# The mixer of a two-layer hybrid decoder: TensorE's order written out while tracing, 64-row scores in pairs

## The chip, the cores and the metric

The kernel runs on one NeuronCore of one Trainium2 chip. The metric is device time in microseconds (us) of one execution. PE is TensorE, PEld its weight loads, DVE VectorE, ACT ScalarE, POOL GpSimd and SP SyncE, whose queue issues most of the transfers.

## What is computed

Two layers on a residual stream of 512 positions by 1024 features in float32; each has a SwiGLU feed-forward stage (FFN), a token mixer and a second FFN, all with RMSNorm and a shift, scale and gate from a conditioning vector. The reference, cut:

```python
for l in range(DEPTH):                              # DEPTH = 2
    h = modulate(rms_norm(x, norm_g[l, 0]), sh1, sc1)
    x = x + 0.5 * g1 * swiglu(h, w_ffn_gu[l, 0], w_ffn_down[l, 0])      # 1024 -> 2 x 2816 -> 1024
    h = modulate(rms_norm(x, norm_g[l, 1]), sh2, sc2)
    x = x + g2 * token_mixing(h, w_in[l], w_out[l], ...)
    h = modulate(rms_norm(x, norm_g[l, 2]), sh3, sc3)
    x = x + 0.5 * g3 * swiglu(h, w_ffn_gu[l, 1], w_ffn_down[l, 1])
return rms_norm(x, final_norm_g)

def token_mixing(h, ...):
    (hq, hf, hi, hg, aq, ak, av, iq, ik, iw, sz, sxbc, sdt) = split(h @ w_in)
    o_a = hgrn2_mixer(hq, hf, hi, hg, ...)          # 4 heads of 64, gated linear recurrence
    o_b = dsa_mixer(aq, ak, av, iq, ik, iw, ...)    # 8 index heads pick the 128 best keys of each query, 4 heads attend
    o_c = mamba2_mixer(sz, sxbc, sdt, ...)          # conv of 4 taps, 8 heads of 64, state 128
    return concatenate([o_a, o_b, o_c]) @ w_out     # 256 + 256 + 512 features
```

## The kernel before

The stream lives in SBUF as eight tiles `X[f]` of 128 features by 512 positions. A dense product is split for accuracy (`mm3`, L304): operands are cut into a high part (`hi`, the rounded type fp32r) and the rest (`lo`), and PE sums hi·hi, lo·hi and hi·lo, three matmuls of 512 columns per 128 by 128 weights. `weights` (L294) loads a chunk of 1024 columns on SP's queue (`wraw`), ACT copies `whi`, DVE subtracts `wlo` (L301); three buffers of each.

Each stage begins with `lead` (L254): two chunks are multiplied by the not yet normalised stream (`xhi`, `xlo`), while the sum of squares is formed; behind product k = `KR[0]` PE sums it over partitions (`msps`), behind `KR[1]` it spreads the result (`rsb`, copied to `rb`). DVE then makes, tile by tile, `ht` = X·gain·rb (L283) and the low part `hlo` (L289), ACT the high part `hhi` (L284). The shift of the two chunks comes as a separate vector: DVE sums eight weight blocks, each by its shift column, into `shw` (L261), and PE reduces it (`pb`, L274).

`mixer` (L444) multiplies by 18 feature-major chunks of `winF` (`fm`, tile `pf`: query 0–1, index query 2–5, forget 6–7, hgrn query 8–9, conv input 10–17) and by position-major groups `winB`, `winV`, `winG`, `winC` (`tm_group`, tile `pt`). Around these:

- *topk* (L536): index scores `ipl`, 24 matmuls with 64 rows each, ACT's Relu, DVE's weighted sum into `iacc` (L550); then 3 x 16 rounds of MAX8 and MATCH_REPLACE8 on DVE.
- *hgrn* (L606): diagonal scores `ldg`, then seven levels of block size 64 to 1. A level makes two tiles `lev` (one for each 128 features; DVE, exponential on ACT, products on POOL) and 16 matmuls `lsc` of 64 rows and 128 columns (L667): four blocks of positions for each head half `par` and tile `f`, in four PSUM tiles; DVE copies them under a mask into `asc` (L669). The two heads of a tile lie in its rows 0–63 and 64–127; `par` is the outer loop, so four matmuls on the same half follow each other.
- *attend* (L743): for each block j of 128 queries and each head a 64-row score `apl`, maximum on DVE, exponential on ACT, transposes `apt`, product `apo`.
- *ssd* (L781): decays (`prow`, `mt`: eight Relu pieces, L839), outputs (`pyd`, `pyo`, `pst`); then `ysplit` (transposes `pyt`) and `project` (`po`).

`zipped` (L729) merges the generators by fixed fractions; that sets priorities, and a list scheduler with a cost model then decides the order on each engine, on PE too, apart from the lead. PSUM has eight banks: three for `mm`, three for `sm`, two for `hm`. `SLOTS` counts the SBUF buffers of each kind.

## Time and profile before

| | us |
|---|---|
| median of 3 runs | 2138.05 |
| lowest and highest run | 2138.03, 2138.57 |
| span of the profiled execution | 2136.6 |

| stretch of layer 0 (us of the span) | what runs |
|---|---|
| 48–404 | first FFN, end of the start-up |
| 399–412 | lead of the mixer, under the last products of the FFN and its own |
| 412–487 | winB, rotations, first chunks of winF |
| 487–610 | levels, index scores, top-k, conv input |
| 610–678 | gates, attention, state space part |
| 678–715 | end of attention and of the state space part, last projection |
| from 715 | second FFN |

Layer 1 has its mixer from 1442.5 to 1758.5. The profiled execution's own time is its span and what lies around it; the table of the runs gives the whole. Of the page, read the busy shares and the chain first, then the timeline of a stretch; busy time of PE is modelled from the starts of its matmuls, so that starts are the safer number. In the rows a matmul of float32 operands stands as two passes, so that a block of eight is x16.

### The profile page before, as it was taken

To read this page: it belongs to the slowest core of one execution; us is meant where nothing else is said; L and a number is where in the kernel's file an instruction comes from. 1 tells how busy PE (TensorE), PEld (TensorE's weight loads), DVE (VectorE), ACT (ScalarE), POOL (GpSimd) and SP (SyncE) were. 2 spreads that over 40 slices of the span, in tenths; PEclk is the share of its full clock that TensorE was granted. 3 is DMA by queue.
4 is the path that set the end of the run, shared out by engine and by line. 5 is a ranking of instruction groups with operands and counts; after the bars stand their busy time and mean duration, and the time that the engine had idled before them with its cause. 6 is when DMAs were issued, how large, how long until landed. Compare 5 with 4: busy or idle time off the path is not lost.

```text
span 2136.6 us, 26813 instructions
## 1 busy us (share of the span) xinstructions
PE 2084.7 (98%) x10201; PEld 1724.8 (81%) x10201; DVE 1304.8 (61%) x2540; ACT 817.7 (38%) x1245; POOL 201.1 (9%) x178
## 2 busy tenths in 40 slices
PE   4999999999999999999999999999999999999998
PEld 3888888887888788888888888888779877888886
DVE  8766564769986877433476743357699775333333
ACT  4422223455564532222342222234655644222233
POOL 4000000112221200000100000011123120000001
PEclk9999999999999999999999999999999999999999
DMA  8556563432110367432346743233311023233322
GB/s 307 204 194 234 179 209 89 128 104 65 58 31 15 121 204 263 129 99 84 94 139 222 273 155 99 78 106 110 94 55 43 16 72 99 90 88 114 94 84 73
DMA packets 103537, 262.51 MB, mean 123 GB/s; under 512 B 12272, under 2 KB 14960, under 8 KB 103408
## 3 DMA queue, kind: packets, MB, share of 16 engines
q1 hardware_dynamic: 100016, 256.60, 37.6%
q10 hardware_dynamic: 3392, 4.20, 0.7%
q8 instruction: 80, 1.31, 0.3%
q14 instruction: 49, 0.40, 0.1%
HBM read 255.50 MB, written 2.10 MB: 121 GB/s over the span
## 4 chain that ended last, share of the span: by engine, by line
PE 94%; DVE 4%; DMA 1%; issue 1%; ACT 1%; SPq 0%; DVEq 0%; ACTq 0%
PE pd L305 7%; PE pd L307 7%; PE pd L306 7%; PE pg L305 7%; PE pu L307 7%; PE pg L306 7%; PE pu L305 7%; PE pu L306 7%; PE pg L307 7%; PE pf L305 3%; PE pf L307 3%; PE pf L306 3%; PE lsc L667 3%; PE pt L469 2%; PE pt L471 2%; PE pt L470 2%
## 5 line engine op out<-in xcount | busy, mean ns | idle before, releaser
L300 ACT ACTIVATE whi<-wraw 128x1024 fp32r<-128x1024 f32 (+2 forms) x374 | 356.7, 957 | 978.3 <-issue 335.2
L301 DVE TENSOR_TENSOR wlo<-wraw,whi 128x1024 fp32r<-128x1024 f32 (+2 forms) x374 | 412.3, 1103 | 389.1 <-ACT whi L300 387.7
L306 PE MATMUL pd<-alo,whi 128*128 128x512 f32 (+1 forms) x715 | 275.8, 386 | 0.0
L307 PE MATMUL pd<-ahi,wlo 128*128 128x512 f32 (+1 forms) x715 | 275.8, 386 | 0.0
L305 PE MATMUL pd<-ahi,whi 128*128 128x512 f32 (+1 forms) x715 | 275.5, 386 | 0.0
L307 PE MATMUL pu<-hhi,wlo 128*128 128x512 f32 x664 | 258.6, 390 | 1.6 <-DVE wlo L301 1.6
L305 PE MATMUL pu<-hhi,whi 128*128 128x512 f32 x664 | 258.7, 390 | 0.2
L305 PE MATMUL pg<-hhi,whi 128*128 128x512 f32 x664 | 258.6, 390 | 0.0
L306 PE MATMUL pu<-hlo,whi 128*128 128x512 f32 x664 | 258.4, 389 | 0.0
L307 PE MATMUL pg<-hhi,wlo 128*128 128x512 f32 x664 | 258.3, 389 | 0.0
L306 PE MATMUL pg<-hlo,whi 128*128 128x512 f32 x664 | 258.3, 389 | 0.0
L160 DVE SCALAR_TENSOR_TENSOR adaw<-adaw,crow 128x512 f32<-128x512 f32 x288 | 193.2, 710 | 5.2 <-DMA adaw<-wada 5.0
L199 POOL TENSOR_TENSOR sq<-sq 128x512 f32<-128x512 f32 x36 | 53.9, 1496 | 1421.4 <-ACT sq L195 1421.2
L396 DVE TENSOR_TENSOR a<-a,pu 128x512 f32<-128x512 f32 x85 | 58.4, 687 | 201.6 <-PE pu L307 201.6
L307 PEld LDWEIGHTS pd<-ahi,wlo 128*128 128x128 f32 x715 | 134.3, 188 | 27.1
L306 PEld LDWEIGHTS pd<-alo,whi 128*128 128x128 f32 x715 | 134.3, 188 | 27.0
L305 PEld LDWEIGHTS pd<-ahi,whi 128*128 128x128 f32 x715 | 134.3, 188 | 27.0
L307 PEld LDWEIGHTS pu<-hhi,wlo 128*128 128x128 f32 x664 | 124.7, 188 | 28.7 <-DVE wlo L301 2.9
L305 PEld LDWEIGHTS pu<-hhi,whi 128*128 128x128 f32 x664 | 124.6, 188 | 27.1 <-ACT whi L300 1.5
L307 PEld LDWEIGHTS pg<-hhi,wlo 128*128 128x128 f32 x664 | 124.6, 188 | 26.0
L305 PEld LDWEIGHTS pg<-hhi,whi 128*128 128x128 f32 x664 | 124.7, 188 | 25.8
L306 PEld LDWEIGHTS pu<-hlo,whi 128*128 128x128 f32 x664 | 124.6, 188 | 25.8
(305 smaller groups left out, 3361.1 us busy)
## 6 DMA issues: line engine op xcount, KB each, us to landing
wraw<-wgu SPq DMA_DIRECT2D x176, 512.0 KB, 3.6
adaw<-wada SPq DMA_DIRECT2D x288, 256.0 KB, 5.0
wraw<-wdn SPq DMA_DIRECT2D x64, 384.0 KB, 3.1
wraw<-wdn SPq DMA_DIRECT2D x64, 320.0 KB, 2.9
wraw<-winF SPq DMA_DIRECT2D x36, 512.0 KB, 3.6
wraw<-woutB SPq DMA_DIRECT2D x16, 384.0 KB, 3.1
wraw<-winC SPq DMA_DIRECT2D x8, 512.0 KB, 3.6
rope<-rraw ACTq DMA_DIRECT2D x48, 64.0 KB, 3.8
```

The source lines that it names most:

```text
L160: V.scalar_tensor_tensor(raw, raw, 1.0, crow[:, h], op0=OP.mult, op1=OP.mult, accum_out=part[:, c, h:h + 1])
L199: (eng if f < NF - 1 else V).tensor_add(ssq_t["t"][:, h], ssq_t["t"][:, h], sq[:, h])
L300: ACT.activation(hi, raw, AF.Copy)
L301: V.tensor_sub(lo, raw, hi.bitcast(F32))
L305: PE.matmul(ps, wh, xh, start=first, stop=False)
L306: PE.matmul(ps, wh, xl, start=False, stop=False)
L307: PE.matmul(ps, wl, xh, start=False, stop=last)
L396: V.tensor_mul(a, a, pu)
L469: PE.matmul(o, hh[kk][:, blk(b)], wh[:, wk], start=first, stop=False, **g)
L470: PE.matmul(o, hl[kk][:, blk(b)], wh[:, wk], start=False, stop=False, **g)
L471: PE.matmul(o, hh[kk][:, blk(b)], wl[:, wk], start=False, stop=last, **g)
L667: PE.matmul(ps[:, blk(b)], xl[f][ph, blk(b)], xl[f][ph, blk(b)], start=True, stop=True)
```

## The change

It touches the mixer, its lead and the pools; the products and their number stay as they are.

- **PE's order.** The whole mixer is under a manual schedule of PE (`mixer_woven`). `weave` runs one generator `dense()` and five chains (`topk`, `hgrn`, `attends`, `ssd`, `select`). A chain yields the time at which it may go on; `clk` advances by the issued PE time (`tick`, 0.681 per `mm3`). `need` waits for marks with latencies, `need_pair` for a PSUM pair; a chain that is due goes ahead of the dense products. The clock is used while tracing only; on the chip PE runs the list in its order.
- **Dense order.** Forget and hgrn query ('h'), winB and index queries ('i'), queries ('q'), winV ('v'), conv ('c'), then winC0, winC1, winG and woutA.
- **Pairs.** `pair` is a tile of two PSUM banks, two buffers; `mm` and `sm` go to two banks each, `hm` goes. `head_pair` sends the matmuls of rows 0–63 and 64–127 alternately into the two banks; `ipl` and `apl` do the same with two or four heads.
- **Merged tiles.** `lev`, `lf`, `kf`, `hq`, `bf`, `kd`, `asc` hold both feature tiles, [128, 2, 512]; a level takes one set of vector instructions.
- **Engines.** `wlo` of 12 winF chunks (`GF`) moves to POOL. The weighted sum of the index scores is ACT scaling plus POOL addition. The lead's `shw` is a POOL product of the whole chunk and one DVE reduction. `KR` goes to (4, 5), in all stages.
- Smaller: state tiles cleared once, norms per block, first level copied by ACT, the start's tiles, a smaller DMA scratch ring.

```diff
-KR = (3, 4)
+KR = (4, 5)
...
-ZD, ZH, ZQ, ZC, ZG = (0.18, 0.59), (0.04, 0.86), (0.04, 0.63), (0.06, 0.79), (0.89, 0.94)
+SPACE = 1.6
+LEVLAT = 9.0
+ATTLAT = 10.0
...
+DORD = 'hiqvc'
...
+SLOTS = {"H": 16, "A": 14, "B": 9, "C": 18}
 WBUF = 3
+GF = (6, 7, 8, 9, 10, 11, 12, 13, 14, 15, 16, 17)
...
         def sm(name, shape=(P, S)):
-            return pq.tile(list(shape), F32, name=name, tag="sm", bufs=3)
-
-        def hm(name, shape=(P, S)):
-            return pq.tile(list(shape), F32, name=name, tag="hm", bufs=2)
+            return pq.tile(list(shape), F32, name=name, tag="sm", bufs=2)
+
+        def pair(name):
+            return pq.tile([P, 2, S], F32, name=name, tag="pair", bufs=2)
...
             with tc.high_priority(WAHEAD):
                 for wh, wl, raw in ws:
-                    t = act("A", "shw", shape=(P, P))
-                    V.tensor_scalar(t, raw[:, blk(0)], shift_of(l, i, 0), None, op0=OP.mult)
-                    for q in range(1, NF):
-                        V.scalar_tensor_tensor(t, raw[:, blk(q)], shift_of(l, i, q), t, op0=OP.mult, op1=OP.add)
-                    ts.append(t)
+                    r4 = raw.rearrange("p (a b m) -> p a b m", a=4, b=2)
+                    GP.tensor_tensor(r4, r4,
+                                     mod[l][:, i * 6:i * 6 + 4, 1::2][:, :, :, None].to_broadcast([P, 4, 2, P]),
+                                     op=OP.mult)
+                    r = act("A", "shw", shape=(P, P))
+                    V.tensor_reduce(r, raw.rearrange("p (q m) -> p m q", q=NF), axis=AX.X, op=OP.add)
+                    ts.append(r)
...
-        def weights(src, n, keep=False):
+        def weights(src, n, keep=False, eng=None):
...
                 ACT.activation(hi, raw, AF.Copy)
-                V.tensor_sub(lo, raw, hi.bitcast(F32))
+                (eng or V).tensor_sub(lo, raw, hi.bitcast(F32))
...
+        def weave(dense, chains):
+            when = lambda e: e[0]() if callable(e[0]) else e[0]
+            src, todo = [0.0, dense], [[0.0, g] for g in chains]
+            while src or todo:
+                live = todo + ([src] if src else [])
+                e = next((e for e in live if when(e) <= clk[0]), None)
+                if e is None:
+                    e = min(live, key=when)
+                    assert when(e) < math.inf
+                    clk[0] = when(e)
+                r = next(e[1], e)
+                if r is not e:
+                    e[0] = r if callable(r) else clk[0] + (r or 0.0)
+                elif e is src:
+                    src = None
+                else:
+                    todo.remove(e)
+
         def mm3(ps, wh, wl, xh, xl, first, last):
+            tick(0.681)
             PE.matmul(ps, wh, xh, start=first, stop=False)
             PE.matmul(ps, wh, xl, start=False, stop=False)
             PE.matmul(ps, wl, xh, start=False, stop=last)
...
+            iqp = pair("pq")
+            iqp = [iqp[:, c] for c in range(2)]
             hh, hl, sb, rb = lead(l, 1, [weights(A["winF"][l, 2 + c], 1024, True) for c in range(2)], iqp)
+            with tc.manual_schedule(engines={mybir.EngineType.PE}):
+                mixer_woven(l, nxt, iqp, hh, hl, sb, rb)
+
+        def mixer_woven(l, nxt, iqp, hh, hl, sb, rb):
...
+            b3 = lambda t: t.rearrange("p (b t) -> p b t", b=NB)
+
+            def mark(k, lat):
+                at[k] = clk[0] + lat
+
+            def need(*ks):
+                return lambda: max(at.get(k, math.inf) for k in ks)
+
+            def need_pair(t=0.0):
+                return lambda: max(t, min(pfree))
+
+            def hold_pair(lat):
+                pfree[pfree.index(min(pfree))] = clk[0] + lat
 
...
                 ps = mm("pf")
                 for k in range(NF):
                     mm3(ps, wh[:, blk(k)], wl[:, blk(k)], hh[k], hl[k], k == 0, k == NF - 1)
+                    yield
                 return ps
...
+            def dense():
+                hold_pair(16.0)
+                for c in DORD:
+                    yield from dict(h=d_forget, i=d_index, q=d_query, v=d_value, c=d_conv)[c]()
                 sz[:] = [act("C", "sz") for _ in range(NB)]
                 for half in range(2):
-                    pC = tm_group(f"winC{half}", 256, 4)
...
+                sg[:] = [act("C", "sg", shape=(P, 2, 256)) for _ in range(2)]
+                yield from tm_group("winG", 256, 4, lambda bp, pp: ACT.activation(sg[bp], pp, AF.Silu))
+                mark("sg", 2.0)
+                yield from first_out()
...
+                        for i in range(hs):
+                            ph = slice(i % 2 * 64, i % 2 * 64 + 64)
+                            PE.matmul(pl[:, i % 2, i // 2 * n:i // 2 * n + n], iqr[(h + i) // 2][ph, blk(j)],
+                                      ikT[ph, :n], start=True, stop=True)
+                        tick(0.2 + n * hs / 1200)
+                        hold_pair(2.5)
...
+                            rl = act("A", "irl")
+                            ACT.activation(rl[:, :hs // 2 * n], pl[:, u, :hs // 2 * n], AF.Relu)
+                            for i in range(hs // 2):
...
+                                r = rl[:, i * n:i * n + n]
+                                if h + i + u == 0:
+                                    ACT.activation(acc[:, :n], r, AF.Copy, scale=w)
+                                else:
+                                    ACT.activation(r, r, AF.Copy, scale=w)
+                                    GP.tensor_tensor(acc[:, :n], acc[:, :n], r, op=OP.add)
...
+            def head_pair(name, kx, qx):
+                ps = pair(name)
+                for b in range(NB):
+                    for u in range(2):
+                        ph = slice(u * 64, u * 64 + 64)
+                        PE.matmul(ps[:, u, blk(b)], kx[ph, blk(b)], qx[ph, blk(b)], start=True, stop=True)
+                tick(1.15)
+                hold_pair(HOLD)
+                return ps
...
+                    for f in range(2):
+                        yield need_pair(ready + 2.0 * f)
+                        ps = head_pair("lsc", xl[:, f], xl[:, f])
+                        if m == 64:
+                            ACT.activation(b8(Asc[f])[:m, :, m:], b8(ps)[:m, :, m:], AF.Copy)
+                        else:
+                            w = lambda t: t.rearrange("p f (g u m) -> p f g u m", u=2, m=m)[:, :, :, 1]
+                            mk = masks[:, li].rearrange("p (g m) -> p g m", m=m)
+                            V.copy_predicated(w(Asc[f]), mk[:, None].to_broadcast([P, 2, S // (2 * m), m]), w(ps))
+                        if f == 0 and li + 1 < len(LEVELS):
...
+                        pl = pair("apl")
+                        for i in range(hs):
+                            ph = slice(i % 2 * 64, i % 2 * 64 + 64)
+                            PE.matmul(pl[:, i % 2, i // 2 * n:i // 2 * n + n], aqr[(h0 + i) // 2][ph, blk(j)],
+                                      akT[ph, :n], start=True, stop=True)
...
-                    px = mm("pxs")
+                    yield need_pair(clk[0] + 2.0)
+                    pr = pair("prow")
+                    for g in range(2):
+                        for r in range(4):
+                            h = g * 4 + r
+                            PE.transpose(pr[:, g, blk(r)], acs[:, b, h:h + 1].to_broadcast([P, P]), ident)
+                    tick(0.9)
+                    hold_pair(4.0)
+                    yield need_pair()
...
+            chains = dict(t=topk, h=hgrn, a=attends, s=ssd)
+            weave(dense(), [chains[c]() for c in ORD] + [select()])
```

Where instructions stand now. PE behind the lead of the first mixer, before and then after (`pb` is the shift sum, `pt` here winB, `pf` a winF chunk):

```order
L307 MATMUL pf<-xhi,wlo 128x512
L274 MATMUL pb<-ones,shw 128x1 x2
L469 MATMUL pt<-whi,hhi 128x208
L470 MATMUL pt<-whi,hlo 128x208
L471 MATMUL pt<-wlo,hhi 128x208
```

```order
L346 MATMUL pq<-xhi,wlo 128x512
L289 MATMUL pb<-ones,shw 128x1 x2
L344 MATMUL pf<-hhi,whi 128x512
L345 MATMUL pf<-hlo,whi 128x512
L346 MATMUL pf<-hhi,wlo 128x512
...
L542 MATMUL pt<-whi,hhi 128x208
```

Ninety-six winF products (four chunks of 24) now stand where winB's began; winB comes behind them.

PE at the level of block size 64, before and then after (`lsc` level scores, `ipl` index scores, `pf` and `pt` dense products):

```order
L305 MATMUL pf<-hhi,whi 128x512
L667 MATMUL lsc<-lev 128x128 x4
L543 MATMUL ipl<-kT,rope 128x384 x2
L667 MATMUL lsc<-lev 128x128 x4
L306 MATMUL pf<-hlo,whi 128x512
L307 MATMUL pf<-hhi,wlo 128x512
```

```order
L544 MATMUL pt<-wlo,hhi 128x208
L749 MATMUL lsc<-lev 128x128 x8
L344 MATMUL pf<-hhi,whi 128x512
L345 MATMUL pf<-hlo,whi 128x512
L346 MATMUL pf<-hhi,wlo 128x512
L749 MATMUL lsc<-lev 128x128 x8
```

Eight level scores on alternate halves stand together, three dense products lie between the two blocks of a level, and index scores stand elsewhere.

POOL from the last level on, before and then after (`kf`, `hq` hgrn key and query, `iacc` index sums, `wlo` low part of winF chunks, `dsd` a diagonal of the state space part):

```order
L660 TENSOR_TENSOR lev<-lev,hq 128x256
L678 TENSOR_TENSOR kf<-kf,lev 128x512
L684 TENSOR_TENSOR hq<-hq,bf 128x512
L816 TENSOR_SCALAR dsd<-ident,vec_77 128x128 x4
...
L706 MEMSET hst 128x128 x5
```

```order
L316 TENSOR_TENSOR wlo<-wraw,whi 128x1024
L720 TENSOR_TENSOR iacc<-iacc,irl 128x384
L804 TENSOR_TENSOR kf<-kf,lev 128x1024
L806 TENSOR_TENSOR hq<-hq,bf 128x1024
L720 TENSOR_TENSOR iacc<-iacc,irl 128x384
L316 TENSOR_TENSOR wlo<-wraw,whi 128x1024
L720 TENSOR_TENSOR iacc<-iacc,irl 128x384 x3
L721 TENSOR_TENSOR iacc<-iacc,cst 128x128
```

Additions of the index scores and subtractions of weights alternate on POOL, and the products for `kf` and `hq` stand between them.

PE near the end of attention (j = 3), before and then after (`apo` attention output, `apl` scores, `prow` and `pxc` decays, `py` and `pyd` state space output, `po` the projection):

```order
L765 MATMUL apo<-kv,pT 128x64 x4
L750 MATMUL apl<-kT,rope 128x512
L836 MATMUL prow<-ident,acs 128x128 x8
L306 MATMUL po<-ylo,whi 128x512
L307 MATMUL po<-yhi,wlo 128x512
...
L307 MATMUL po<-yhi,wlo 128x512
L848 MATMUL pyd<-dsd,xbc 128x128
L851 MATMUL pyd<-xdt,mt 128x64 x2
```

```order
L916 MATMUL apo<-kv,pT 128x64 x8
L885 MATMUL apl<-kT,rope 128x512 x2
L977 MATMUL prow<-ident,acs 128x128 x8
L984 MATMUL pxc<-ident,xbc 128x128 x4
L988 MATMUL pxc<-xbc 128x128 x2
L993 MATMUL pxc<-ident,xbc 128x128 x2
L1017 MATMUL py<-dsd,xbc 128x128
L1020 MATMUL py<-xdt,mt 128x64 x2
```

The decays of a block and its output now follow each other with no dense product between them; `prow`, `pxc` and `py` are three users of the two pairs.

## Rows read from the trace of the kernel before

**Rows 1.** The page: busy time and share of the span, granted clock, chain by engine.

```profile
PE 2084.7 (98%) x10201; PEld 1724.8 (81%) x10201; DVE 1304.8 (61%) x2540; ACT 817.7 (38%) x1245; POOL 201.1 (9%) x178
...
PEclk9999999999999999999999999999999999999999
...
PE 94%; DVE 4%; DMA 1%; issue 1%; ACT 1%; SPq 0%; DVEq 0%; ACTq 0%
```

**Rows 2.** PE's timeline (start, us, line, operation): mixer 0's ends, its sums of squares.

```profile
399.25 0.39 PE L305 MATMUL pf<-xhi,whi 128*128 128x512 f32 x1
...
403.33 0.95 PE L227 MATMUL msps<-ones,sq 128*128 128x1 f32 x8
...
715.34 0.39 PE L305 MATMUL pg<-xhi,whi 128*128 128x512 f32 x1
```

**Rows 3.** Stretches: us, busy PE, PEld, DVE, ACT, POOL, clock, DMA share, GB/s.

```profile
404.00:487.00 83.00, 81.82 (x464) 70.75 (x464) 53.89 (x105) 45.88 (x63) 11.01 (x7) 1.00 0.35 104
487.00:610.00 123.00, 122.97 (x759) 99.54 (x756) 120.80 (x293) 68.93 (x114) 34.02 (x36) 1.00 0.19 55
...
678.00:723.00 45.00, 42.20 (x195) 33.10 (x194) 36.97 (x57) 20.82 (x31) 11.53 (x7) 1.00 0.29 89
```

**Rows 4.** The chain of waits (start us, us, what), score blocks on PE.

```profile
487.38 0.88 PE ldg L645 x8
...
532.85 1.98 PE lsc L667 x16
...
614.52 0.84 PE apl L750 x2
...
639.81 1.05 PE apl L750 x2
```

**Rows 5.** Timeline of PE, and of weight loads (PEld): passes on both and one half.

```profile
486.68 0.70 PE L543 MATMUL ipl<-kT,rope 64*128 64x256 f32 x4
...
525.40 0.19 PEld L667 LDWEIGHTS lsc<-lev 64*128 64x128 f32 x1
525.40 0.19 PEld L543 LDWEIGHTS ipl<-kT,rope 64*128 64x128 f32 x1
...
608.44 0.70 PE L750 MATMUL apl<-kT,rope 64*128 64x256 f32 x2
```

**Rows 6.** PE's timeline at one level block.

```profile
532.46 0.40 PE L306 MATMUL pf<-hlo,whi 128*128 128x512 f32 x1
532.78 2.05 PE L667 MATMUL lsc<-lev 64*128 64x128 f32 x16
```

**Rows 7.** Timeline behind the lead of mixer 0: DVE, PE and POOL.

```profile
408.49 0.75 DVE L289 SCALAR_TENSOR_TENSOR hlo<-ht,mod,hhi 128x512 fp32r<-128x512 f32 x1
...
409.83 0.75 DVE L289 SCALAR_TENSOR_TENSOR hlo<-ht,mod,hhi 128x512 fp32r<-128x512 f32 x1
...
411.94 0.35 PE L469 MATMUL pt<-whi,hhi 128*128 128x208 f32 x1
...
413.35 0.28 PE L469 MATMUL pt<-whi,hhi 128*128 128x208 f32 x1
...
421.67 1.78 POOL L486 TENSOR_TENSOR rraw<-rraw,cst 128x512 f32<-128x512 f32 x1 [16.09 <-DMA rope<-rraw]
...
422.22 1.78 DVE L289 SCALAR_TENSOR_TENSOR hlo<-ht,mod,hhi 128x512 fp32r<-128x512 f32 x1
```

**Rows 8.** Groups by line and form (busy us, mean ns): DVE from 404 to 746, POOL overall.

```profile
L301 DVE TENSOR_TENSOR wlo<-wraw,whi 128x1024 fp32r<-128x1024 f32 x31 | 38.4, 1238 | 15.1 <-ACT whi L300 15.1
L669 DVE COPY_PREDICATED asc<-masks,lsc 128x256 f32<-128x256 uint8 x28 | 14.3, 510 | 0.9 <-PE lsc L667 0.9
...
L550 DVE SCALAR_TENSOR_TENSOR iacc<-irl,kv,iacc 128x512 f32<-128x512 f32 x7 | 5.5, 780 | 0.0
...
L362 POOL TENSOR_TENSOR wlo<-wraw,whi 128x512 fp32r<-128x512 f32 x4 | 6.0, 1531 | 11.8 <-ACT whi L361 11.8
```

**Rows 9.** The same view of ScalarE, from 404 to 746.

```profile
L839 ACT ACTIVATE mt<-prow,acs 128x128 f32<-128x128 f32 x32 | 9.1, 379 | 3.0 <-PE prow L836 3.0
```

715 lines of the change are left out of this document (391 added, 324 removed).

## The prediction

> **What bounds the kernel now.** I read the page first. TensorE (PE) is busy 98% of the span at the upper of its two clocks (2.4 GHz: 9 tenths or more granted in every slice, 1.00 in the stretches of [rows 3]), and the chain that ended last is 94% PE [rows 1]. So the time is a queue of matmuls, and only a change in PE's time or in PE's waits can show. Next the timeline of PE, to cut out one mixer: from its first product to the first product of the FFN behind it 715.34 - 399.25 = 316.1 us [rows 2]; the second mixer is the same code on other weights, so every term below counts twice. The 18 products from 399.25 to the sum of squares at 403.33 give the price of a dense product of 512 columns, 0.227 us. Then the table by stretch: from 404 to 610 PE idles 1.2 us of 206, and VectorE (DVE) is busy 120.80 of the 123 us in which the levels and the top-k run, while GpSimd (POOL) has 34 of them [rows 3]. Thus PE has almost no waits to remove. DVE only just keeps up there.
>
> **What is removed from PE.** A score matmul works on 64 of the 128 rows. The chain shows what one block of eight costs when it stands alone: 1.98 us for 16 passes (each such matmul is two), and the attention scores 0.84 us for 384 columns and 1.05 us for 512 [rows 4]. Do two on opposite halves run side by side? The timeline shows it by chance: four 256-column index passes, of two heads that use the two halves, take 0.70 us, and two passes of one half take 0.70 us too; and at 525.40 two weight loads of the two halves start together [rows 5]. After the change every head pair alternates halves. Per mixer:
> - level scores: 7 levels x 16 matmuls = 14 blocks of eight, 14 x 1.98 = 27.7 us, halved: -13.9;
> - diagonal scores: 16 matmuls, four runs of 0.88, 3.5 us, halved: -1.8;
> - attention scores: 16 matmuls, four heads each of 1.05 and 0.84 us, and of 0.6 and 0.4 for 256 and 128 columns (an estimate: in proportion 0.55 and 0.27, and something for the ends), 11.6, halved -5.8, less 0.3 for ends that stay: -5.5;
> - index scores: 24 matmuls, 20 us if each stood alone, but most already stand beside another (first row of [rows 5]); half of what is left, an estimate: -3.5 (2 to 10 by how many do);
> - a block between dense products costs more than its passes: the block follows the product before it after 0.32 instead of 0.227 us [rows 6], and as much again is lost behind it. The new order has ten blocks fewer, of 0.2 us at most: -1.6 (an estimate).
>
> Sum -26.3, and PE's small waits inside the old mixer (1 us) go too: **-27.3 per mixer**. The number of dense products is the same, so nothing else leaves PE.
>
> **What is added: waits of PE.** The order on PE is now fixed while tracing, by a clock that counts issued PE time and fixed latencies. PE cannot go round a late producer any more, so each lateness is paid in full. I cost four places.
>
> (1) Behind the lead. Before, the products of winB (208 columns) followed `pb`, twelve per k in 413.35 - 411.94 = 1.41 us, while DVE made one pair ht/hlo per 1.34 us (hlo starts 408.49 and 409.83) [rows 7]. Both ran at the same pace, and PE hardly waited. Now 96 products of the forget and query columns follow, 3 x 0.227 = 0.68 us per k. The chain starts 1.36 us later too, since KR moves `rsb` by one k, six matmuls of 0.227. So hlo(7) lands near 408.49 + 0.75 + 1.36 + 7 x 1.33 = 419.9, and PE wants it at 411.9 + 7 x 0.68 = 416.7: 3.2 us at least. On ACT the hi copies of the next weights stand between the hhi: two of 1.05 us; and chunks 7 and 8 have their lo part on POOL, beside DVE's hlo. Lower bound 2.2 (ACT makes good one k of it), upper 8 (as late as before, when the hlo at 422.22 ended at 424.0): I take 5.5, between the pure chain and the upper end.
>
> (2) Diagonals and pairs. There are two pair buffers. The lead's `pq` holds one until DVE has read it, and that read now stands behind a rotation that waits for a transfer and POOL: 1 (0 to 2). In the levels a buffer comes free when DVE's masked copy of 2 x 256 columns is done, 2 x 0.51 us [rows 8], twice per level; with the top-k in DVE's queue: 2.5 (0 to 8, from a DVE at 98% in that stretch [rows 3]).
>
> (3) The conv stage. 12 of the 18 winF chunks get their lo part on POOL. POOL takes 1.53 us for 512 columns [rows 8], 3.06 for a chunk, where DVE took 1.24 (31 of them in one mixer). A chunk on PE is 8 x 0.68 = 5.4 us, so POOL keeps pace if it has little else; it now also has the 21 adds of the index scores, at 0.8 to 1.5 us in proportion: 1.5 (0 to 6).
>
> (4) The tail. Attention for j = 3, the decays of the state space part, `pyt` and the last projection share two pair buffers, and ACT runs eight Relu pieces of 0.38 us per block [rows 9] before a `prow` buffer is free. PE order there is fixed, with few dense products between: 4.5 (2 to 9). The old tail idled 45.0 - 42.2 = 2.8 us [rows 3], some of which is the lead of the FFN.
>
> Sum 5.5 + 1 + 2.5 + 1.5 + 4.5 = **15** (4 to 33).
>
> **What leaves DVE** is hidden and pays only by keeping these waits small: 12 x 1.24 = 14.9 us of wlo, 24 accumulates, the widest of 0.78 (17.7 by their three widths) [rows 8], and most of the shift products: some 36 us per mixer. POOL gets 12 x 3.06 = 37 of wlo, 24 of adds and 6 of shift products, 67 us. FFN stages: the shift sum moves to POOL and one reduction, with one k more in hand; I take 0 (-3 to +3 for all), hidden under the lead's 48 products of 0.227. ACT does 24 scalings more, copies the first level's scores and has fewer function tables to load; the state tiles are cleared once, the norms are taken per block, tiles are merged in pairs, and the software DMA ring is smaller: all beside PE, 0. The weights are asked for in the new order on SP's queue; the DMA engines are busy 0.35 and 0.19 of the time in these stretches [rows 3], so a chunk is early either way: 0; uncovered, one chunk late costs what its transfer takes past its 5.4 us on PE.
>
> **Sum.** -27.3 + 15 = -12.3 per mixer, twice: -24.6. The profiled span 2136.6 becomes 2112.0; outside it lie 2138.05 - 2136.6 = 1.45 us to the median of the runs. Forecast **2113.5 us**.
>
> **Rivals.**
> *Waits nearly gone.* If DVE, 36 us lighter, is always ahead, and the clock's latencies were large enough, 5 us of waits remain (mostly place 1): -22.3 x 2, 2093.5. For it: DVE's release. Against: at place 1 the pace 1.33 against 0.68 is in the rows.
>
> *POOL holds DVE up (slower).* In the lead, while POOL multiplies `rraw` (421.67 to 423.45, 1.78 us), DVE's hlo at 422.22 takes 1.78 instead of 0.75 us [rows 7]: two engines that read SBUF together slow each other down. The Trainium skill, "SBUF — State Buffer", Who interferes with whom, has a rule for this: a DVE instruction with two SBUF inputs and a GpSimd instruction that reads SBUF exclude each other for a whole instruction, and it speaks against moving half of DVE's work to POOL. Worked out from rows: in the stretch of 123 us DVE drops from 120.8 to about 93, while PE's time there falls by 22 to 101. The added 61 us of wlo and adds on POOL hold DVE in half of their time: 93 + 30 = 123, 22 us beyond PE. With 11 us of the lead and the tail, 33 us of waits: +5.7 x 2, **2149.5**. It decides from 27 us of waits on. Against: MAX8 and MATCH_REPLACE8, a large part of DVE's work there, read one wide tile only, while the row shows the slowing for an operation that reads two; and the top-k has all the conv stage to end in.
>
> *The pairs don't pair.* If 128-column passes are bound by something that the halves share, only the wide ones gain: -27.3 + 15.7 = -11.6, plus 15: +3.4 x 2, 2145. Against: the loads that start together, and passes of one half beside another's [rows 5].
>
> *Gain eaten.* Waits of 25 to 29: within 0.2% of before.
>
> **How the numbers follow.** Chances: forecast 0.52, waits nearly gone 0.27, gain eaten 0.08, POOL holds DVE 0.09, pairs don't pair 0.04. A measurement of this kernel can tell some 0.2%, 4.3 us. Faster than 2133.8: 0.52 + 0.27 and none of the rest, and a part of the forecast's own spread that reaches into no change, 0.01, goes to same: faster 0.78, same 0.09, slower 0.13. For the range: waits of 4 give 2136.6 - 46.6 + 1.45 = 2091.5, less up to 3 us of FFN: 2088; above, it takes in the eaten gain to 2138; the two slow rivals, 0.13, stay out.
>
> **What would show it.** In the new profile `lsc` blocks of eight matmuls last 1.0 us instead of 1.98; the two mixers, from first to first product, 304 us each; PE waits for hlo or hhi in the 96 products behind the lead, 3 to 8 us per mixer, and for DVE or ACT releases of pairs in the tail; wlo on POOL at 3.06 us or more; the FFN stages unchanged. Wrong it is if blocks of eight still take 1.7 us or more, if a mixer waits under 8 or over 25 us, or if the FFN stages move by over 3 us.

## The result and the profile after

| | before | after |
|---|---|---|
| median of four runs (us) | 2138.05 | 2167.75 |
| lowest to highest run | 2138.03–2138.57 | 2164.86–2173.37 |
| profiled span | 2136.6 | 2166.1 |
| mean granted clock of PE in it | 0.998 | 0.984 |

The ratio is 1.0142, interval [1.0127, 1.0156]: the changed kernel is slower, by 29.7 us or 1.4%. The forecast was 2113.5, its range ended at 2138.0; the time lies outside, on the other side of no change. The runs of after also spread more, 0.4% against 0.03%.

The page after (busy time, granted clock, chain by engine), against [rows 1]:

```profile
PE 2070.3 (96%) x10201; PEld 1711.5 (79%) x10201; DVE 1300.9 (60%) x2338; ACT 825.1 (38%) x1249; POOL 324.0 (15%) x232
...
PEclk9999999999999999999999999999999999999999
...
PE 74%; DVE 14%; ACT 4%; POOL 3%; issue 3%; DMA 2%; ACTq 1%; SPq 0%; POOLq 0%; DVEq 0%
```

PE's share of the chain falls from 94% to 74%, DVE's rises from 4% to 14%: the end is no longer set by a queue of matmuls alone. DVE's busy time is the same as before (1300.9 against 1304.8), though some 70 us of its work had been meant to leave it; POOL has 123 us more. The tenths of the clock row hide the loss of clock; the table by stretch below shows it.

PE's timeline at the ends of the first mixer, as in [rows 2]:

```profile
402.35 0.39 PE L344 MATMUL pq<-xhi,whi 128*128 128x512 f32 x1
...
732.13 0.39 PE L344 MATMUL pg<-xhi,whi 128*128 128x512 f32 x1
```

That is 329.8 us instead of 316.1; the second mixer takes 329.5 instead of 316.0. These two differences, 13.7 and 13.5, are 27.2 of the 29.5 us of span. The rest of the program adds 2.3: 3.1 up to the first mixer, 0.4 between the mixers, 1.2 less behind the second.

The stretches of the first mixer (us, busy PE, PEld, DVE, ACT, POOL, granted clock, DMA share, GB/s), against [rows 3]:

```profile
402.00:420.00 18.00, 16.41 (x77) 12.47 (x75) 13.65 (x16) 7.53 (x10) 10.04 (x5) 1.00 0.27 87
420.00:446.00 26.00, 23.55 (x100) 18.89 (x100) 16.96 (x28) 17.51 (x22) 6.15 (x4) 0.87 0.36 105
446.00:484.00 38.00, 38.00 (x299) 32.22 (x298) 32.70 (x45) 14.71 (x22) 19.83 (x14) 1.00 0.29 77
484.00:550.00 66.00, 55.25 (x351) 40.09 (x350) 55.75 (x113) 35.98 (x62) 46.68 (x34) 0.92 0.21 56
550.00:612.00 62.00, 58.20 (x339) 50.41 (x337) 57.55 (x146) 38.95 (x71) 21.31 (x16) 0.94 0.20 60
612.00:665.00 53.00, 51.14 (x391) 48.25 (x392) 31.78 (x69) 35.39 (x77) 3.18 (x4) 0.94 0.16 48
665.00:732.00 67.00, 64.09 (x331) 52.98 (x330) 47.75 (x68) 29.61 (x57) 15.32 (x13) 0.97 0.16 50
```

PE idles 10.75 us of the 66 in which levels and index scores run, and only one stretch (446 to 484) has neither idle time nor a clock below 1.00. Before, PE idled 1.2 us from 404 to 610, at 1.00 [rows 3]. What it waits for in this mixer (us in total, times, longest):

```profile
PE ipl L706 <- DVE asc L795: 5.9, 2, 4.0
PE lsc L749 <- ACT irl L712: 3.9, 4, 1.5
PE pf L345 <- DVE hlo L304: 3.8, 2, 2.4
PE prow L977 <- ACT dec L965: 3.2, 1, 3.2
PE hps L831 <- ACT yhg L856: 1.5, 1, 1.5
...
```

The pairs do pair. A block of eight level scores (the chain had 1.98 us in [rows 4]) now stands so in PE's timeline:

```profile
507.42 1.16 PE L749 MATMUL lsc<-lev 64*128 64x128 f32 x16 [1.54 <-ACT irl L712]
```

Two 128-column passes, one on each half, now start together every 0.105 us, where one pass started every 0.112 us.

**The sum of one mixer.** Each matmul of the trace counts with the time from its start to the next start; two passes that start together on the two halves count as one step. The price of a step is the median of its kind at full clock. What a step in a stretch of granted clock 0.5 takes beyond its price, up to that price once more, counts as half clock; of what is then left, anything over 0.25 us counts as a wait, and the rest as switching between kinds. First mixer, us:

| | before | after | difference |
|---|---|---|---|
| medians of all matmuls, and switching | 313.3 | 289.5 | -23.8 |
| waits | 2.8 | 26.4 | +23.6 |
| half clock | 0.0 | 13.9 | +13.9 |
| together | 316.1 | 329.8 | +13.7 |

The second mixer gives -23.3, +26.5 and +10.3. As a bound on the last row: PE is busy for 30.2 us of the stretches at half clock in the first mixer and for 21.5 us in the second. Dense products start every 0.43 us there and every 0.227 us at full clock, so the clock can have cost some half of that at most, 15.1 and 10.7 us.

### The profile page after: what moved, and what is told of

It reads as the page before. It is cut to its first block, busy times and chain, and to the rows that moved or that the text cites. A ratio compares the mean times of both kernels' runs of the same rounds, so it can differ in the third digit from the quotient of the medians.

```text
span 2166.1 us, 26665 instructions
## 1 busy us (share of the span) xinstructions
PE 2070.3 (96%) x10201; PEld 1711.5 (79%) x10201; DVE 1300.9 (60%) x2338; ACT 825.1 (38%) x1249; POOL 324.0 (15%) x232
## 4 chain that ended last, share of the span: by engine, by line
PE 74%; DVE 14%; ACT 4%; POOL 3%; issue 3%; DMA 2%; ACTq 1%; SPq 0%; POOLq 0%; DVEq 0%
PE pg L344 7%; PE pu L346 7%; PE pg L345 7%; PE pu L344 7%; PE pu L345 7%; PE pg L346 7%; PE pd L345 7%; PE pd L344 7%; PE pd L346 7%; DVE xbc L655 2%; DVE iacc L735 2%; DVE m L732 1%; DVE wlo L316 1%; ACT whi L315 1%; PE po L345 1%
## 5 line engine op out<-in xcount | busy, mean ns | idle before, releaser
L315 ACT ACTIVATE whi<-wraw 128x1024 fp32r<-128x1024 f32 (+1 forms) x374 | 357.2, 957 | 978.0 <-issue 363.4
L316 DVE TENSOR_TENSOR wlo<-wraw,whi 128x1024 fp32r<-128x1024 f32 (+2 forms) x350 | 388.6, 1111 | 371.5 <-ACT whi L315 370.1
L212 POOL TENSOR_TENSOR sq<-sq 128x512 f32<-128x512 f32 x36 | 48.7, 1353 | 1409.3 <-ACT sq L208 1409.1
L345 PEld LDWEIGHTS pg<-hlo,whi 128*128 128x128 f32 x656 | 123.1, 188 | 26.7 <-DVE hlo L304 1.0
```

What stands on the lines that cost most here:

```text
L212: (eng if f < NF - 1 else V).tensor_add(ssq_t["t"][:, h], ssq_t["t"][:, h], sq[:, h])
L315: ACT.activation(hi, raw, AF.Copy)
L316: (eng or V).tensor_sub(lo, raw, hi.bitcast(F32))
L345: PE.matmul(ps, wh, xl, start=False, stop=False)
```

## The experiments

The question is why 24 us of saved matmul time per mixer bring 24 to 27 us more of waits, and 10 to 14 us of half clock on top. My theory after the result: PE's list is fixed, so the mixer is a chain through DVE, ACT and POOL that no longer has dense products in the right places, and local causes add up. Rivals: POOL alone holds DVE up; DVE's throughput (the top-k) is the bound; the tracing clock's constants are wrong; the pairs themselves hurt. The times below are medians, each ratio goes against runs of before that were taken together with that kernel, and the mixers are those of the one profiled execution.

| kernel | us | ratio to before | mixers (us) |
|---|---|---|---|
| before | 2138.05 | | 316.1, 316.0 |
| after | 2167.75 | 1.0142 [1.0127, 1.0156] | 329.8, 329.5 |
| e1_pool_undone | 2163.37 | 1.0116 [1.0099, 1.0133] | 328.4, 330.5 |
| e2_forget_interleaved | 2166.97 | 1.0133 [1.0118, 1.0148] | 331.4, 330.6 |
| e5_filler | 2170.35 | 1.0153 [1.0134, 1.0171] | 329.0, 336.0 |
| e4_before_paired | 2149.90 | 1.0053 [1.0038, 1.0068] | 322.4, 321.4 |
| e3_levels_unpaired | 2174.86 | 1.0173 [1.0158, 1.0188] | 331.4, 333.9 |
| e6_after_half_topk | 2163.40 | 1.0120 [1.0105, 1.0135] | 326.8, 333.8 |
| e8_before_half_topk | 2150.14 | 1.0056 [1.0039, 1.0073] | 321.3, 322.6 |
| e7_before_paired_half_topk | 2133.28 | 0.9982 [0.9972, 0.9991] | 312.3, 314.8 |
| e9_long_latencies | 2209.34 | 1.0332 [1.0317, 1.0348] | 350.2, 349.5 |
| e18_short_latencies | 2194.11 | 1.0259 [1.0244, 1.0274] | 341.6, 340.8 |
| e13_index_first | 2208.50 | 1.0330 [1.0313, 1.0347] | 349.0, 350.8 |
| e14_index_first_long_lat | 2219.72 | 1.0379 [1.0363, 1.0394] | 352.7, 361.4 |
| e16_index_first_pool_undone | 2216.32 | 1.0364 [1.0348, 1.0379] | 353.7, 353.0 |
| e19_made_wait | 2189.72 | 1.0237 [1.0222, 1.0252] | 340.1, 340.6 |
| e17_before_pool_moves | 2176.35 | 1.0176 [1.0161, 1.0192] | 335.2, 334.8 |
| e8_dt_later | 2155.70 | 1.0084 [1.0068, 1.0101] | 324.7, 323.3 |
| e21_dt_later_wlo_dve | 2155.79 | 1.0085 [1.0068, 1.0102] | 323.9, 323.7 |
| e20_dt_later_pool_undone | 2148.46 | 1.0047 [1.0032, 1.0062] | 318.8, 319.6 |

### POOL's work undone in the new order

```diff
-GF = (6, 7, 8, 9, 10, 11, 12, 13, 14, 15, 16, 17)
+GF = ()
...
-                                    ACT.activation(r, r, AF.Copy, scale=w)
-                                    GP.tensor_tensor(acc[:, :n], acc[:, :n], r, op=OP.add)
+                                    V.scalar_tensor_tensor(acc[:, :n], r, w, acc[:, :n], op0=OP.mult, op1=OP.add)
```

> The changed kernel, with the low parts of the 12 winF chunks and the sum of the index scores back on DVE; order of PE and pairs as changed. Theory (POOL holds DVE, both on a fixed PE order): the waits of PE for masked copies and for index pairs between the levels, some 12 us per mixer with the clock that falls behind them, shrink by more than half though DVE has 32 us more to do: 2140 to 2152 us against 2167.8. Rival (DVE simply has too much to do, or the latencies of the clock are too short): the waits stay or grow, 2168 us or more.

Measured 2163.4, between the two ranges: 4 us under after, whose own runs spread over 8.5 us. The waits are as large as with the moves (28.2 and 31.7 us per mixer, 26.4 and 29.3 in after). By itself POOL's new work is not the cause. The edit also takes the 24 scalings of the index scores off ACT, some 12 us of its busy time per mixer.

### The wait behind the lead

In one kernel the two forget chunks are interleaved by k, so that twice as many products stand behind each `hlo`; in the other, three matmuls per k that nothing reads fill the wait.

```diff
...
+                for k in range(NF):
+                    for f in range(2):
+                        wh, wl = ws[f]
+                        mm3(pss[f], wh[:, blk(k)], wl[:, blk(k)], hh[k], hl[k], k == 0, k == NF - 1)
...
```

> The changed kernel, with the products of the two forget chunks behind the lead interleaved k by k (the second in an sm bank), so that PE asks for a new pair hhi/hlo every 1.36 us instead of every 0.68. Theory: the two waits for hlo behind the lead (4.6 us per mixer) and the half clock that follows them (3.3 us in mixer 0) go: 12 to 16 us less in all, 2152 to 2156 us. Rival: the levels start later by what they gained and wait elsewhere: 2165 to 2170.

```diff
...
+                    if c == 6 and k < NF - 1:
+                        for _ in range(3):
+                            PE.matmul(dm, wh[:, blk(k)], hh[k], start=True, stop=True)
```

> The changed kernel with 42 matmuls more: behind each of the first seven product triples after the lead, three of 512 columns that nothing reads, 4.8 us per mixer, in the place where PE waits 4.6 us for hlo. If the granted clock falls because PE waited there: the stretch of 6.8 us at half clock from 420.8 on is gone, and the time is 0 to 4 us less in spite of the added work, 2163 to 2168. If the clock falls for another reason: it still falls, and the time stays or rises by up to 5 us, 2168 to 2173.

2167.0 and 2170.4. Interleaved, the wait for `hlo` is gone, and the diagonals wait instead:

```profile
PE ldg L756 <- DVE rraw L554: 6.1, 2, 3.1
```

That is the total of both mixers. The wait moved down the chain; the time stayed. The filler shortened the stretch at half clock behind the wait (3.41 us instead of 6.83 in both mixers), but its total lies within the spread of after, so it decides nothing.

### The pairs alone, and the top-k

The kernel before with alternate halves in `ldg` and `lsc` only; and after with the halves in a row again:

```diff
...
-                    for par in range(2):
-                        ph = slice(par * 64, par * 64 + 64)
-                        for f in range(2):
-                            ps = hm("lsc")
-                            for b in range(NB):
+                    for f in range(2):
+                        pp = [hm("lsc") for par in range(2)]
+                        for b in range(NB):
+                            for par in range(2):
+                                ph = slice(par * 64, par * 64 + 64)
...
```

> The kernel before, with one edit: the diagonal and level scores of the two head halves alternate, in the two banks of hm; scheduler, engines and pools as before. If PE's time bounds it: 15.7 us less per mixer, 2105 to 2110 us. Rival (DVE, 98% busy in the stretch of the levels, is the next bound there, so that PE's gain comes back as waits): 2128 to 2138.

```diff
-                for b in range(NB):
-                    for u in range(2):
+                for u in range(2):
+                    for b in range(NB):
```

> The changed kernel with the eight matmuls of each level and diagonal block sent half by half (four on rows 0 to 63, then four on 64 to 127) instead of alternately. PE then works 15 us longer per mixer. Theory (between the lead and the last masked copy a chain of DVE, POOL, ACT and transfers sets the time, and PE waits in it): the time stays, 2163 to 2175 us. Rival (PE's own time sets it, the waits are extra): 2190 to 2200 us.

Pairing alone made the old kernel slower, 2149.9. Its matmuls and switching take 8 us less per mixer, half of what was expected: level and diagonal scores take 11.6 us less, index scores 3.1 more. And the list scheduler lays out another order, waits go from 3 to 13 us, and some 4 us of half clock come in; two of the waits (first mixer) and the clock behind the first:

```profile
PE apt L763 <- ACT pexp L759: 4.0, 2, 3.2
PE pyt L919 <- DVE ylo L923: 2.2, 1, 2.2
```

```profile
540.00:558.90 18.90, 14.78 (x86) 11.12 (x84) 18.67 (x49) 13.86 (x21) 3.40 (x4) 1.00 0.29 85
558.90:566.00 7.10, 7.10 (x40) 6.43 (x40) 7.10 (x21) 6.46 (x11) 1.67 (x2) 0.52 0.26 74
```

Taken out of after, the level pairs cost 8.5 us per mixer on PE (medians and switching; 15 were expected), 17 in all, and the time rose by only 7, since the waits shrank by 3 to 7 us per mixer. So more than half of what these pairs save comes back, as waits and half clock, in both of these kernels.

Is it DVE's throughput? Three kernels with half of the selection rounds, in after, in before, and in before with pairs (the edit as it stands in before):

```diff
-                        V.max(m8, acc[:, :n])
-                        V.match_replace(acc[:, :n], m8, acc[:, :n], GONE)
+                        if r < TOPK // 16:
+                            V.max(m8, acc[:, :n])
+                            V.match_replace(acc[:, :n], m8, acc[:, :n], GONE)
```

> The changed kernel with 8 instead of 16 rounds of MAX8 and MATCH_REPLACE8 for each block of queries; order of PE unchanged. It leaves out half of the selection, some 28 us of DVE per mixer. Theory (DVE's queue sets the time from the index scores to the decays): 12 to 25 us less per mixer, 2118 to 2144 us. Rival (the fixed order and its two pair buffers set it, whatever DVE does): 2160 to 2168.

> The kernel before with half of the selection rounds left out and nothing else. If PE's time bounds the kernel before: 2134 to 2138 us, though DVE has 28 us less per mixer. If DVE bounded it already: 2100 to 2125.

> The kernel before with paired diagonal and level scores and half of the selection rounds left out. Theory (pairing gains PE time that DVE's queue gave back): 8 us or more per mixer less than the kernel before with half the rounds, so 2110 to 2122 us. Rival (pairing itself costs, by the order that the scheduler finds): as with all rounds, 2142 to 2150.

In after, 23 us less busy DVE per mixer bought 4 us, again within the spread: DVE's load is not the bound. In before, less work was even slower (2150.1, outside both ranges); the scheduler's order changed with it, and that this made it slower is argued, not shown. There pairing is worth 17 us (2150.1 to 2133.3), with almost no half clock. The same edit gave +12 us with the whole selection and -17 us with half of it, each in an order of its own. So whether the gain is kept depends on the work beside it or on the order; the two were not taken apart.

### The tracing clock's constants, and the order of the dense work

```diff
-LEVLAT = 9.0
-ATTLAT = 10.0
-IDXLAT = 3.6
-HOLD = 3.5
+LEVLAT = 13.0
+ATTLAT = 12.0
+IDXLAT = 5.0
+HOLD = 6.0
```

(the long one, which also lengthens `MTLAT`, `KDLAT` and the latencies written inside the chains; the short one takes 0.7 of these four, of `MTLAT` and of `KDLAT`)

> The changed kernel with longer latencies in the clock that writes PE's order: pairs held 6.0 instead of 3.5 and 2.5 us, a level 13 instead of 9, an index step 5.0 instead of 3.6, the decays 8 instead of 2, others by a third. More dense products then lie between the scores, and fewer are left for the end. Theory (PE waits because the order expects DVE, POOL and ACT sooner than they come): the 13 us of waits between 484 and 550 fall below 5; the tail, which has fewer dense products, waits 3 to 8 us more; 2145 to 2160 us. Rival (the waits follow the vector work wherever the dense products stand): the waits stay, 2163 to 2172.

> The changed kernel with the six fixed latencies of the tracing clock (pair held, level, index score, attention, decays, kd) times 0.7, so that the chains' matmuls stand earlier on PE among the dense products. Longer ones gave 2209. Theory 'the list on PE sets the time, and each lateness is paid': matmuls that stand earlier wait longer, but the chain ends earlier and leaves dense products for the tail: between 2150 and 2185, waits of PE in the levels over 20 us per mixer. If the latencies are merely too short as they are: over 2185. If they are too long as they are: under 2150.

2209.3 (above both ranges) and 2194.1: worse on both sides, so the theory that the constants of after are merely too short or too long falls, as far as two kernels can show it. Longer ones push the chain behind the dense work, and PE waits for single steps of it (both mixers):

```profile
PE lsc L749 <- DVE asc L795: 24.4, 4, 9.5
```

With the index chunks ahead of the forget chunks, the top-k begins as early as before (497.8 us, in before 496.5, in after 521.0). The second kernel has the long latencies too, the third the undone POOL work; there the top-k begins at 512.6 and 508.1:

```diff
-DORD = 'hiqvc'
+DORD = 'ihqvc'
```

> The changed kernel with the dense order 'ihqvc' in place of 'hiqvc': winB and the index queries ahead of the forget and hgrn query chunks, so that the index scores, and the top-k behind them, start some 20 us sooner. Theory (the late start of the top-k leaves the attention and its latencies in the tail, and puts index scores and levels into one stretch): 8 to 15 us less per mixer, 2138 to 2152 us. Rival (levels and index scores change places, and the waits with them): 2160 to 2172.

> Both edits: longer latencies and the index chunks first. If the two causes add: 2120 to 2140 us, a mixer of 305 to 315 us. If the time is bound by the vector work in any order: 2155 or more.

> Index chunks first, with the low parts and the index sums back on DVE. If POOL holds DVE in the stretch where the top-k runs: 5 to 15 us less than with index chunks first alone. If the 32 us that DVE gets back weigh as much: within 5 us of it.

All three are slower than after, by 41 to 52 us, and above their ranges, except that the second is where its rival had it (2155 or more). A dense product stands behind a PSUM bank that an index chunk holds until ACT has read it, for 17.7 us per mixer in the first, 17.8 in the second and 14.8 in the third. The first:

```profile
PE pf L344 <- ACT rraw L552: 35.4, 2, 17.7
```

ACT comes to it late, because the copy ahead of it in its queue waits for DVE's read of the lead's `pq`. An early top-k is worth nothing if one entry of the list blocks PE for 17.7 us; PE does not pass it.

### A wait made on purpose

Between the two query chunks, where after has neither wait nor low clock, PE transposes a tile, ACT copies it five times, and PE needs the last copy.

```diff
+                for b in range(NB):
+                    PE.transpose(dm[:, blk(b)], iqr[0][:, blk(b)], ident)
+                ACT.activation(wt, dm, AF.Copy)
+                for _ in range(4):
+                    ACT.activation(wt, wt, AF.Copy)
+                PE.transpose(dn[:, :P], wt[:, :P], ident)
```

> The changed kernel with one wait of PE made on purpose, between the two query chunks (near 465 us of the span, where the changed kernel has no wait and the granted clock is 1.00): four transposes, five ScalarE copies of 512 columns, a transpose that needs the last copy, results unused; 3 to 5 us of wait per mixer. Theory 'a wait of PE of some 2 us or more brings a stretch at the lower clock behind it': a stretch of 3.4 or 6.8 us at 0.5 within some 10 us behind the made wait, in both mixers, which costs half its length on top. Rival 'the lower clock belongs to the 64-row blocks or to the load on all engines, not to waits': the clock stays at 1.00 there. Total with the theory 2167 + 2 x (4 to 8), less what the chains behind gain by the delay: 2168 to 2183.

The wait came out longer than meant, 7.83 us. PE's timeline, then the stretches around it (columns as above):

```profile
481.17 0.60 PE L641 MATMUL dm<-ident,rope 128*128 128x128 f32 x4
489.60 0.48 PE L646 MATMUL dm<-ident,wt 128*128 128x128 f32 x1 [7.83 <-ACT wt L644]
...
490.30 0.63 PE L345 MATMUL pf<-hlo,whi 128*128 128x512 f32 x1
```

```profile
460.00:481.00 21.00, 21.00 (x137) 16.84 (x138) 17.42 (x29) 5.87 (x10) 10.91 (x8) 1.00 0.31 89
481.00:485.70 4.70, 0.76 (x6) 0.43 (x4) 3.65 (x5) 2.52 (x4) 2.81 (x2) 1.00 0.49 78
485.70:495.90 10.20, 6.30 (x29) 4.61 (x31) 3.94 (x5) 3.12 (x5) 1.79 (x1) 0.50 0.34 118
495.90:505.00 9.10, 9.10 (x63) 7.21 (x63) 0.72 (x1) 4.44 (x8) 4.58 (x4) 1.00 0.07 16
```

The granted clock falls to 0.50 in the middle of the wait and stays there for 6.3 us of work behind it, which cost some 3 us; in the second mixer the made wait of 7.82 us has a stretch of 6.83 us, 3.3 of them with work, some 1.6 us. So a wait brings the half clock to a place that had none. Together the two mixers are 21.4 us longer than in after, for 15.7 us of made wait. Every one of the ten stretches of half clock in the mixers of after begins in or just behind waits of PE (420.8 behind the `hlo` waits, 513.0 in the 4.0 us for `asc`, 612.0 in the 3.2 for `prow`, and so on).

The reverse does not hold: not every wait brings a stretch. In the second mixer of after PE waits 3.53 us for `dec`, and the granted clock is 1.00 in the wait and behind it:

```profile
1671.71 1.09 PE L977 MATMUL prow<-ident,acs 128*128 128x128 f32 x8 [3.53 <-ACT dec L965]
```

```profile
1668.00:1671.80 3.80, 0.27 (x3) 0.10 (x2) 3.73 (x10) 2.31 (x4) 0.00 (x0) 1.00 0.00 0
1671.80:1690.00 18.20, 18.20 (x151) 17.59 (x152) 17.35 (x38) 13.52 (x27) 0.00 (x0) 1.00 0.19 52
```

What decides between the two is not shown. Over the two mixers of after, 55.7 us of waits came with 24.2 us of half clock.

### Which DVE steps are late: dt, and POOL beside them

The largest single wait of after is `ipl` for `asc` at 514.2. The timeline of DVE and POOL ahead of it:

```profile
506.74 1.48 DVE L947 TENSOR_SCALAR dt<-dt 128x32 f32<-128x32 f32 x1
508.26 1.45 DVE L946 TENSOR_TENSOR dt<-dt,spw 128x32 f32<-128x32 f32 x1
...
511.20 1.42 DVE L946 TENSOR_TENSOR dt<-dt,spw 128x32 f32<-128x32 f32 x1
...
513.47 0.69 DVE L795 COPY_PREDICATED asc<-masks,lsc 128x512 f32<-128x512 uint8 x1
```

```profile
506.68 1.50 POOL L774 TENSOR_TENSOR lev<-lev,kf 128x512 f32<-128x512 f32 x1 [1.72 <-ACT lev L773]
508.14 1.52 POOL L775 TENSOR_TENSOR lev<-lev,hq 128x512 f32<-128x512 f32 x1
...
511.08 1.49 POOL L775 TENSOR_TENSOR lev<-lev,hq 128x512 f32<-128x512 f32 x1
```

```profile
514.22 1.65 PE L706 MATMUL ipl<-kT,rope 64*128 64x384 f32 x4 [4.01 <-DVE asc L795]
```

Each DVE step on 32 columns, 0.18 us by itself, ends with the POOL instruction beside it, after 1.4 us; the masked copy that frees the pair stands behind four of these and a fifth of 0.90 us. In before the same steps began at 437.0, when POOL had almost nothing, at 0.17 to 0.19 us each. So three more kernels: dt started later (one line), the same with all POOL moves undone, and the same with only `wlo` back on DVE. A fourth is before with nothing but the POOL moves.

```diff
             def ssd():
-                yield need("idx1")
+                yield need("idx3")
```

> One line of the changed kernel: the state space chain may start only when the index scores of the last query block are issued, so that the sixteen 128 by 32 vector steps on dt no longer stand on VectorE in front of the masked copies at 507 to 512 us. Theory 'POOL holds VectorE at that place': the 4.0 us wait of ipl for asc and the half clock behind it (513.0, 6.83 us at half speed, 3.4 us lost) go, in both mixers: 2 x 5 to 7 us, 2154 to 2158. Rival 'each wait that goes is replaced by the next in the fixed order': 2163 to 2174, with the wait elsewhere; the dt steps then stand near the tail and prow waits longer for dec.

Measured 2155.7, 12 us under after, as the theory had it. The copy that ended at 514.2 now stands at 506.91, and the wait of 4.0 us is gone; `ipl` waits for `asc` 2.3 us in the first mixer instead of 5.9, while `prow` and `hps` wait longer. The half clock there did not go: its stretch is 3.41 us from 507.6, in place of 6.83 from 513.0.

```profile
506.91 0.71 DVE L795 COPY_PREDICATED asc<-masks,lsc 128x512 f32<-128x512 uint8 x1
```

```profile
PE prow L977 <- ACT dec L965: 4.2, 1, 4.2
...
PE hps L831 <- ACT yhg L856: 3.5, 1, 3.5
PE ipl L706 <- DVE asc L795: 2.3, 1, 2.3
```

> The later start of the dt steps (2155.7 by itself, 12 us under the changed kernel) together with both POOL moves undone (2163.4 by itself, 4 us under it). Theory 'the dt steps hurt because POOL holds them in front of the masked copies': without the POOL work they run in 0.2 us wherever they stand, so the two gains are the same one and do not add: 2153 to 2163. Rival 'two separate gains': 2149 to 2153.

> The later start of the dt steps, with the low parts of the 12 winF chunks back on VectorE (15 us of its time per mixer) and the index sums left on POOL. If the low parts are the POOL work that costs (2.36 us each, 12 per mixer, two VectorE operations held by each): 2140 to 2150. If POOL's work is covered now that the dt steps are gone from the levels: 2153 to 2160, or more where VectorE becomes late with them.

2148.5 and 2155.8. The gains of the later dt and of the undone POOL work add; my theory that they are one effect was wrong. What held the dt steps is `lev`, which POOL had before too; what the POOL moves cost is apart from it. It hangs on the index sums, not on `wlo`: with `wlo` back on DVE nothing changed, with the sums back too it gained 7 us. The wait that falls most is that of `prow` for ACT's `dec`, 2.9 us in both mixers with `wlo` alone back; with the sums back too, in the first mixer (the second has some 0.5, but there `pacs` waits 1.7 us for DVE's `da`):

```profile
PE prow L976 <- ACT dec L964: 0.4, 1, 0.4
```

With the sums go the 24 scalings on ACT, the engine that makes `dec`. Whether POOL's additions or ACT's scalings cost the 7 us was not taken apart.

```diff
-                wh, wl = weights(A["winF"][l, c], 1024)
+                wh, wl = weights(A["winF"][l, c], 1024, eng=GP if c >= 6 else None)
...
-                            V.scalar_tensor_tensor(acc[:, :n], rl[:, :n], w, acc[:, :n], op0=OP.mult, op1=OP.add)
+                            ACT.activation(rl[:, :n], rl[:, :n], AF.Copy, scale=w)
+                            GP.tensor_tensor(acc[:, :n], acc[:, :n], rl[:, :n], op=OP.add)
```

> The kernel before with nothing but the two moves of work to POOL: the low parts of the 12 winF chunks, and the weighted index sums as ScalarE scaling with POOL additions; order, unpaired scores and tiles as before, PE still in the list scheduler's order. If moving work to POOL costs by itself (VectorE held while POOL reads SBUF): 2146 to 2158. If it only bites where a fixed order of PE leaves no way round: 2134 to 2142, the same as before.

2176.4, above both ranges: under the list scheduler the POOL moves alone cost 38 us. Waits go from 3 to some 12 us per mixer, with 5 to 6 us of half clock, and matmuls and switching take 4 us more; the largest wait is

```profile
PE ldg L646 <- ACT hq L631: 3.4, 1, 3.4
```

The expectation that the list scheduler finds a way round was wrong. This kernel differs from before in its whole order too, so its 38 us are the price of the moves together with the order that came of them.

None of the kernels that do all the work beats before.

## Why the prediction was wrong, point by point

**What bounds the kernel** was read rightly for before: a queue of matmuls with 3 us of waits per mixer. That such a queue leaves no slack to the chains beside it was there to be read and not used. DVE at 120.80 of 123 us [rows 3] looked like the chain to wait for; but half of the selection rounds taken out of after, 23 us of DVE per mixer, gave no more than 4 us, so it is not DVE's load that PE waits for.

**What leaves PE: right.** Forecast -27.3, 1 of it old waits; measured -23.8 and -23.3 of matmul time, and 2.8 of old waits. By kind, first mixer: level scores -12.4 (forecast -13.9), diagonals -1.4 (-1.8), attention -5.8 (-5.5), index scores -2.1 (-3.5). Blocks of eight take 1.16 us (forecast 1.0), and the rival that the pairs don't pair is out.

**The sum of the waits and the clock: the step that failed.** Forecast 15 us of waits (4 to 33) per mixer and nothing for the clock; measured 26.4 and 29.3 us of waits, and 13.9 and 10.3 us of half clock. The mixer was to be 12.3 us shorter and came out 13.7 longer in the first. Of these 26.0 us, 11.4 are waits, 13.9 the clock and 0.7 what leaves PE. The waits by themselves lie inside their range; with the clock, 40 us per mixer were lost, beyond its upper end. Term by term, first mixer:

- (1) behind the lead, 5.5 (2.2 to 8): 4.0 measured. Right, and in the place and by the releaser that were named.
- (2) diagonals and pairs, 1 + 2.5 (0 to 10 together): 11.7 from 484 to 550, and 14.2 in the second mixer. The mis-sized term. It was priced as masked copies at 0.51 us behind a busy DVE. What stood ahead of them were the dt steps at 1.4 us, held by POOL, and ScalarE: `lsc` waits for `irl`, because the Relu that frees a pair stands in ACT's queue behind an exponential that waits for DVE's `lev`:

```profile
505.54 1.06 ACT L773 ACTIVATE lev<-lev 128x1024 f32<-128x1024 f32 x1 [1.46 <-DVE lev L772]
506.51 0.85 ACT L712 ACTIVATE irl<-ipl 128x384 f32<-128x384 f32 x2
```

- (3) conv stage, 1.5 for `wlo` on POOL: none for `wlo`, and moving it back changed nothing. A chunk takes POOL 2.35 to 2.41 us there, not 3.06. A wait of 1.7 us of `hps` for `yhg` stands in this stage and in no term.
- (4) tail, 4.5 (2 to 9): 8.6 with the wait of `prow` for `dec` at 609. At the upper end.

**The clock was no term of the sum**, since before showed no half clock inside a mixer. The made wait shows that a wait can bring it. With the clock counted, a microsecond of added wait cost 1.6 us in the first mixer (23.6 + 13.9 over 23.6) and 1.4 in the second.

**"What leaves DVE" did not leave it.** DVE's busy time in the mixer was to fall by some 36 us, and is 256 us in 330 against 255 in 316 before. From the groups by line: index sums -18.0, `wlo` -11.3, shift products -4.4, but `dt` +8.1, `xbc` +3.8, `kv` +4.1, `ht` +2.1, `hss` +2.3 and others. `wlo`, `xbc` and dt of after:

```profile
L316 DVE TENSOR_TENSOR wlo<-wraw,whi 128x1024 fp32r<-128x1024 f32 x17 | 23.4, 1379 | 4.2 <-ACT whi L315 4.2
...
L655 DVE SCALAR_TENSOR_TENSOR xbc<-xraw,vec,xbc 128x510 f32<-128x510 f32 x8 | 7.8, 970 | 0.1
...
L946 DVE TENSOR_TENSOR dt<-dt,spw 128x32 f32<-128x32 f32 x8 | 5.6, 702 | 0.2
L947 DVE TENSOR_SCALAR dt<-dt 128x32 f32<-128x32 f32 x8 | 5.4, 680 | 0.2
```

In the kernel with later dt and POOL's moves undone, `xbc` is 742 ns and dt 181: it is POOL's company that lengthens these two. `wlo` had 1238 ns in [rows 8] and has 1351 in that kernel too, so its length has another cause, which stays open.

**The rival "POOL holds DVE up"** (0.09) had the side right, not the weight. The holding is in the rows, but undoing POOL's moves alone gave 4 us of 29.7, and after is 18 us slower still than this rival's 2149.5. It hurt most where a chain of short steps stood beside POOL's `lev`, which the change did not put on POOL; it put dt beside it. The rule that I weighed was one for operations with two SBUF inputs; here a one-input TENSOR_SCALAR was held as well.

**FFN 0 (-3 to +3):** +2.3 for all. Right in the sum, which hides +3.1 us ahead of the first mixer and -1.2 behind the second.

What is shown: two local causes, dt beside `lev` and the index sums taken off DVE (to ACT and POOL), are worth 19 of 29.7 us. The last 10 stay open: 21 to 24 us of waits and 6 to 8 of half clock are left in the best of these kernels, spread over many places, more than the 23 to 24 us that leave PE. The merged tiles, the smaller PSUM pools and the manual order by itself were not run alone. That the order of PE's list carries the blame for them is argued from the runs in which little but the order changed, and the time rose by 26 to 52 us over that of after; it is not shown wait by wait.

## What to carry to other kernels

In a kernel whose PE is busy 98% of the time, time taken out of PE can come back as waits for the chains beside it, here all of it and more; count the saving as nothing until a wait for each consumer has been priced. With a fixed order, look on each engine's queue for what stands ahead of the one step that PE waits for: short steps beside a POOL instruction take as long as that instruction, and one line that started them elsewhere gave 12 us. Price the half clock with the waits: in after it added 0.4 us for each microsecond of wait on average, though not behind each.
